# Sums of squares accumulated in PSUM, and a first product twice as wide, in a two-layer diffusion backbone

## The chip, the core and the metric

The kernel runs on one core of one Trainium2 chip. The time is device microseconds of one execution. Five engines work side by side, each through its own queue in order: PE (TensorE, matrix products into PSUM), DVE (VectorE), ACT (ScalarE), POOL (GpSimd), and SP (SyncE, which here issues nearly all DMAs). PEld is the loading of PE's stationary operand.

## The reference

Two layers of a transformer over 512 latent and 256 context tokens of width 1024, all in float32. What matters here is the first thing that layer 0 does:

```python
mod = silu_c @ w_mod[l] + b_mod[l]           # and mod_c for the context stream
sh1, sc1, g1, sh2, sc2, g2 = jnp.split(mod[:, None, :], N_MOD, axis=-1)
h = modulate(rms_norm(x, g_norm_attn[l]), sh1, sc1)
proj = h @ w_in[l]   # query latent 256 | kv latent 128 | rope key 32 | sq 512 | sk 128 | sv 128 | dq 512 | dk 512 | dv 512 | gates 3072
```

`rms_norm` divides every token by the root of the mean of its squares over the 1024 features; the columns of `proj` then feed three attention branches (latent attention, windowed attention, differential attention) and three gates. `dv` are the values of the differential branch.

## The kernel before

The residual is kept transposed: eight feature tiles `x[k]` of 128 features by 768 tokens (latent tokens first, context tokens after them). Products run in float32r: each operand is split into a rounded part and a remainder (`hh`, `hl` for the normed tokens, `wh`, `wl` for weights), and three products are summed in PSUM (hi by hi, hi by lo, lo by hi). A piece of weights comes by DMA into one of two slots `wr` (line 194), ACT rounds it into `wh` (line 197) and POOL subtracts to get `wl` (line 199); both stand in four common slots, or in slots of the phase's own.

The first stage (`first_norm`, `first_products`) goes like this.

1. The eight tiles `x[k]` come by DMA. ACT squares each (lines 322 and 392), DVE adds the squares up in one tile `acc` (line 393).
2. PE sums `acc` over its 128 features (`rows_rsq`, line 402): six products `st`, one per block of 128 tokens, each with a whole 128x128 stationary block of `acc` and two columns to move. A float32 product is two instructions in the trace.
3. DVE takes the inverse root in twelve small steps (lines 443 to 454) and puts it on a diagonal, `dg` (line 405). PE spreads it over all partitions (`nr`, line 339), ACT copies that to `rb` (line 340).
4. Shift and scale of the norm come from `silu(c) @ w_mod`, in four quarters of 2 MB of weights (`mod_first`): 32 small products `pm` per quarter (line 266), a copy `me`, a transpose `pmt` (line 274), two additions on DVE (line 295) and the gains `A` (lines 380, 382).
5. For each feature tile k: `nt` on DVE (line 355), `hh` on ACT (line 357), `hl` on DVE (line 358), then 18 products `pq` (lines 205 to 207) of 128x256: six token tiles by three. They give the query latent, which stays in PSUM over all eight k. The quarter `pm` of the next two feature tiles stands ahead of the even k's products, its transpose `pmt` ahead of the odd k's.

Within this stage PE's instructions stand in the order in which the program writes them (`manual_schedule`); everywhere else a list scheduler orders them by its own estimates.

Then comes the projection phase (`phase1`): the copies of the query latent out of PSUM (line 573); the key and value columns in one chunk of 416 columns (`pb`, lines 481 to 483, weights `wkvs`, 144 products); then chunks of 256 columns, one letter each in the string `mcafldebghijnPk`. A chunk is 144 products, followed by norm and rotation on DVE and stores to DRAM. `f`, `l`, `b` and `h` are short ones (18 products each, latent attention's keys and values), `d` and `j` its queries, `e` and `k` the two halves of the differential values. Two eighths of a further modulation (`mod_units`, products `pm`, weights `wm1` by line 306) follow each letter. Everything after that, from the attention on, is not touched.

Of the kernel before, what the change touches and what calls it, by code (L numbers as in the profile page):

```python
"""Two layers of the hybrid diffusion backbone (MLA + windowed GQA + differential attention).

The residual stream is kept transposed (features on partitions, tokens on the free axis, latent
tokens first, context tokens after them).  Products run in float32r: every float32 operand is split
exactly into a rounded part and a remainder, and the three products that matter at float32
accuracy (hi*hi, lo*hi, hi*lo) are accumulated in PSUM.
"""
# [27 lines left out]
# columns of w_in  # L35
C_QLAT, C_KVLAT, C_KPE, C_SQ, C_SK, C_SV, C_DQ, C_DK, C_DV, C_G = (
    0, 256, 384, 416, 928, 1056, 1184, 1696, 2208, 2720)
# rope order of a head: [first halves of row and column | second halves of row and column]
# [3 lines left out]
# broadcast vectors of a layer  # L42
V_MQ, V_MK, V_SQ, V_SK, V_DQ, V_DK, V_SINK, V_L = 0, 96, 192, 256, 320, 384, 448, 456
NV = 456 + 256
# per-partition vectors of a layer
P_GA, P_GM, P_BM, P_GQ, P_GKV, P_GS = 0, 8, 16, 64, 66, 67
NP_ = 68
# constants
# [30 lines left out]
def _layout(inp):  # L79
    """Host side: permutations and concatenations only."""  # L80
# [6 lines left out]
    # units of four feature blocks: shift and scale of the first norm by pairs of feature tiles, then kinds 2, 4 and 3  # L87
# [49 lines left out]
class Build:  # L137
    def __init__(self, tc, ins, out):
        self.tc = tc
        self.nc = tc.nc  # L140
        self.ins = ins
        self.out = out
        self.n = 0
        self.mq = []
        self.early = False
        self.gains = {}
        self.F1, self.WD, self.WC = 0.3, 1.5, 0.4   # how the gates are spread over the attention
        self.px = 0

# [11 lines left out]
    def R(self, name, dt=F32):  # L161
        """a [128, 768] tile of the phase's pool"""
        return self.ph.tile([128, 768], dt, tag="R", bufs=self.NR, name=self.nm(name))
# [7 lines left out]
    def psx(self, name):  # L171
        """one bank for a dense product, from both tags in turn"""
# [16 lines left out]
    def piece(self, src, n=1024, own=0):  # L189
        """hi, lo of a piece of weights; own: the number of slots it takes of the phase's pool in place of the common  # L190
        ones."""
# [10 lines left out]
    def mm3(self, out, ah, al, bh, bl, start, stop):  # L202
        """out += (ah + al).T @ (bh + bl) but for al.T @ bl."""
# [9 lines left out]
    def dense_steps(self, ps, w, x, c):  # L213
        """ps = sum of w.T @ x[:, c]; w: [(hi, lo)] stationary [128, 128] blocks, x: [(hi, lo)] moving."""
# [8 lines left out]
    def split_sb(self, src, n=768):  # L223
        """hi, lo of an SBUF tile."""
# [7 lines left out]
    def mod_start(self, kinds):  # L232
        """queue up mod = silu(c) @ w_mod + b_mod for the given sixths, features on partitions."""
# [27 lines left out]
    def mod_pe(self, w, ks, ps):  # L261
        """ps[32 g + stream, 128 features] += 2 silu(c) @ w for four feature blocks g; w [128, len(ks), 512]."""
# [7 lines left out]
    def mod_out(self, ps, pt):  # L270
        """[128 features, 4 blocks, 32]: twice the modulation without its bias."""
# [5 lines left out]
    def mod_first(self, q):  # L277
        """shift and scale of the first norm for feature tiles 2q and 2q + 1, in two steps."""
# [18 lines left out]
    def mod_units(self, n):  # L297
        """n pieces of the modulation of kinds 2, 4 and 3 of the first layer."""
# [18 lines left out]
    def first_norm(self, x, h):  # L317
        """the first norm, feature tiles as their modulation arrives, and the query latent of the first layer: PSUM
        tiles [128 tokens, 256]."""
        nc = self.nc  # L320
        acc = self.S("acc0")
        first = nc.scalar.activation(out=acc, in_=x[0], func=AF.Square)
        with self.tc.issue_after(first.ins):
            for k in range(1, KT):
                self.add_square(acc, x[k], k, slice(0, 768), self.P("sq"), nc.vector)
        with self.tc.manual_schedule(engines={mybir.EngineType.PE}):
            return self.first_products(x, h, acc)

    def first_products(self, x, h, acc):
        nc = self.nc  # L330
        g0 = self.mod_first(0)
        next(g0)
        dg = self.rows_rsq(acc, NT, self.kc[:, K_O1024:K_O1024 + 2])
# [7 lines left out]
        w = self.wpieces([self.ins["wb"][0, 0, i] for i in range(2)], 4, 256, 2)  # L341
        out = []
        for _ in range(2):
            t = self.psS("pq")
            out += [t[:, 0:256], t[:, 512:768]]
        out += [self.psd("pq")[:, 0:256] for _ in range(2)]
        for q in range(4):
            nxt = self.mod_first(q + 1) if q < 3 else iter(())
            for k in (2 * q, 2 * q + 1):
                next(nxt, None)  # L350
# [9 lines left out]
                for i in range(NT):  # L360
                    b = slice(i * 128, i * 128 + 128)
                    self.mm3(out[i], h[k][0][:, b], h[k][1][:, b], *w[k], k == 0, k == KT - 1)
        return out

    def norm_gain(self, l, which, s, k=None):
        """128 * g * (1 + scale) per feature (rows_rsq gives 1 / 128); of feature tiles k and k + 1 alone at every even k."""
# [19 lines left out]
    def add_square(self, acc, x, j, c, sq, eng):  # L386
        """acc += x_j ** 2 on columns c; sq: a scratch tile."""
# [7 lines left out]
    def rows_rsq(self, sq, nt, ones, s=None):  # L395
        """sq [128 features, nt * 128 tokens] of squares -> [128, nt * 128]: rsqrt(mean + eps) of the tokens on the
        diagonal of every block, with eps * s ** 2 if the rows are s times too large. ones: column constant 1 / number
        of features."""
        nc = self.nc
        st = self.psm("st")  # L400
        for t in range(nt):
            nc.tensor.matmul(st[:, 2 * t:2 * t + 2], lhsT=sq[:, t * 128:t * 128 + 128], rhs=ones, start=True, stop=True)
# [1127 lines left out]
```

## Time and profile before

| | |
|---|---|
| timed runs | 2545.8, 2549.3, 2554.59 us; median 2549.3 |
| span of the profiled execution | 2547.0 us, 40061 instructions |
| PE, PEld busy | 2432.5 us (96%), 2136.6 us (84%) |
| DVE, ACT, POOL busy | 1537.6 us (60%), 1079.7 us (42%), 915.1 us (36%) |
| PE busy in the first of 40 slices | six tenths; nine tenths or more in nearly all others |
| DMA in the first slice | 280 GB/s, against a mean of 121 GB/s |

The profiled execution's own time beyond its span is not listed; its span is 2.3 us under the median of the timed runs. A busy time of PE is the sum of stretches in which an instruction was under way; since products overlap, how many start in a stretch says more than the busy share. The column PEclk is the granted TensorE clock as a share of 2.4 GHz (0.50 is 1.2 GHz).

### The profile page before, as it was taken

The numbers are of one execution on the slowest core, as the hardware profiler recorded it, in microseconds if no ns is written. First come the engines' busy times: TensorE is split into PE (matmuls) and PEld (weight loads), VectorE is DVE, ScalarE is ACT, GpSimd is POOL, SyncE is SP. The second block draws the span as 40 slices with busy tenths as digits, with TensorE's granted clock in tenths as the row PEclk, the third lists the DMA queues.
The fourth block names the chain that finished last, engine by engine and source line by source line (L and its number), as shares of the span: only waits on it lengthen the run. The fifth ranks groups of instructions, "written<-read, shape, count | busy, mean of one in ns | idle before, by whom it ended". The sixth has DMA issues, their size and how long they took to land. (4 is left out here: it accounts for less than half of the span.)

```text
span 2547.0 us, 40061 instructions
## 1 busy us (share of the span) xinstructions
PE 2432.5 (96%) x15466; PEld 2136.6 (84%) x15466; DVE 1537.6 (60%) x3081; ACT 1079.7 (42%) x2105; POOL 915.1 (36%) x629
## 2 busy tenths in 40 slices
PE   6999999999999998999999989999999999999999
PEld 5989888888888887888888989998878777888888
DVE  6547777878874479872222277777788874621112
ACT  4343566667652233212222244346666632422321
POOL 2434211111115326434333354441222235454543
PEclk9999999999999999999999999999999999999999
DMA  7265322222346225662111122443323344222222
GB/s 280 90 222 203 131 97 84 96 77 94 100 137 226 94 76 171 214 231 75 59 67 66 60 99 86 173 153 95 103 83 118 110 156 155 83 92 99 91 100 83
DMA packets 133182, 307.38 MB, mean 121 GB/s; under 512 B 43264, under 2 KB 49536, under 8 KB 132608
## 3 DMA queue, kind: packets, MB, share of 16 engines
q1 hardware_dynamic: 122624, 281.23, 32.6%
q10 hardware_dynamic: 10368, 23.60, 2.4%
q8 instruction: 122, 2.00, 0.3%
q14 instruction: 68, 0.56, 0.1%
HBM read 252.08 MB, written 52.70 MB: 120 GB/s over the span
## 5 line engine op out<-in xcount | busy, mean ns | idle before, releaser
L199 POOL TENSOR_TENSOR wl<-wr,wh 128x1024 fp32r<-128x1024 f32 (+2 forms) x266 | 652.6, 2457 | 1139.2 <-ACT wh L197 1066.8
L197 ACT ACTIVATE wh<-wr 128x1024 fp32r<-128x1024 f32 (+2 forms) x266 | 279.5, 1052 | 581.2 <-PE mo L219 317.6
L218 PE MATMUL mo<-uh,wh 128*128 128x512 f32 (+1 forms) x832 | 286.4, 344 | 18.6 <-DVE x L1261 13.6
L219 PE MATMUL mi<-hl,wh 128*128 128x512 f32 (+1 forms) x832 | 285.7, 344 | 3.3 <-DVE hl L434 3.3
L220 PE MATMUL mi<-hh,wl 128*128 128x512 f32 (+1 forms) x832 | 285.2, 343 | 0.0
L218 PE MATMUL mi<-hh,wh 128*128 128x512 f32 (+1 forms) x832 | 284.8, 344 | 0.3 <-DVE x L1261 0.3
L219 PE MATMUL mo<-ul,wh 128*128 128x512 f32 (+1 forms) x832 | 283.8, 341 | 0.0
L220 PE MATMUL mo<-uh,wl 128*128 128x512 f32 (+1 forms) x832 | 283.1, 341 | 0.0
L1307 DVE TENSOR_TENSOR ul<-u,uh 128x512 fp32r<-128x512 f32 (+1 forms) x104 | 80.7, 777 | 304.0 <-POOL u L1306 301.7
L1261 DVE SCALAR_TENSOR_TENSOR x<-mo,mod,x 128x512 f32<-128x512 f32 (+1 forms) x208 | 127.9, 625 | 200.6 <-PE mo L220 200.6
L481 PE MATMUL pb<-wh,hh 128*128 128x256 f32 (+1 forms) x832 | 244.2, 294 | 0.0
L482 PE MATMUL pb<-wl,hh 128*128 128x256 f32 (+1 forms) x832 | 243.2, 292 | 0.8 <-POOL wl L199 0.8
L483 PE MATMUL pb<-wh,hl 128*128 128x256 f32 (+1 forms) x832 | 243.3, 293 | 0.0
L218 PE MATMUL g<-hh,wh 128*128 128x512 f32 (+1 forms) x576 | 212.2, 368 | 0.0
L220 PE MATMUL g<-hh,wl 128*128 128x512 f32 (+1 forms) x576 | 211.8, 368 | 0.0
L219 PE MATMUL g<-hl,wh 128*128 128x512 f32 (+1 forms) x576 | 211.5, 367 | 0.0
L868 ACT ACTIVATE pth<-pT 128x512 fp32r<-128x512 f32 (+3 forms) x344 | 154.1, 462 | 101.7 <-PE pT L865 90.4
L218 PEld LDWEIGHTS mo<-uh,wh 128*128 128x128 f32 x832 | 157.3, 189 | 39.1 <-DVE x L1261 14.9
L869 DVE TENSOR_TENSOR ptl<-pT,pth 128x512 fp32r<-128x512 f32 (+3 forms) x344 | 171.9, 516 | 24.8 <-ACT pth L868 22.6
L219 PEld LDWEIGHTS mi<-hl,wh 128*128 128x128 f32 x832 | 157.3, 189 | 23.5 <-DVE hl L434 3.7
L218 PEld LDWEIGHTS mi<-hh,wh 128*128 128x128 f32 x832 | 156.8, 189 | 20.4 <-DVE x L1261 0.5
L220 PEld LDWEIGHTS mi<-hh,wl 128*128 128x128 f32 x832 | 157.3, 189 | 19.8
(243 smaller groups left out, 5932.5 us busy)
## 6 DMA issues: line engine op xcount, KB each, us to landing
wr<-in_wmi SPq DMA_DIRECT2D x64, 512.0 KB, 3.5
wr<-in_wmo SPq DMA_DIRECT2D x64, 512.0 KB, 3.5
wm<-in_wmod SPq DMA_DIRECT2D x56, 512.0 KB, 3.6
wr<-in_wg SPq DMA_DIRECT2D x48, 512.0 KB, 3.6
wr<-in_wb SPq DMA_DIRECT2D x36, 512.0 KB, 4.2
wm<-in_wm SPq DMA_DIRECT2D x28, 512.0 KB, 4.5
wr<-in_wup SPq DMA_DIRECT2D x24, 512.0 KB, 3.5
gd<-gt ACTq DMA_DIRECT2D x24, 384.0 KB, 2.4
```

Source lines behind the costliest of these rows:

```text
L197: nc.scalar.activation(out=hi[:, :n], in_=raw[:, :n], func=AF.Copy)
L199: nc.gpsimd.tensor_tensor(out=lo[:, :n], in0=raw[:, :n], in1=hi[:, :n].bitcast(F32), op=ALU.subtract)
L218: mm(ps, lhsT=wh, rhs=xh[:, c], start=i == 0, stop=False)
L219: mm(ps, lhsT=wh, rhs=xl[:, c], start=False, stop=False)
L220: mm(ps, lhsT=wl, rhs=xh[:, c], start=False, stop=i == n - 1)
L481: mm(ps[:, :n], lhsT=ah[:, cs], rhs=wh, start=k == 0, stop=False)
L482: mm(ps[:, :n], lhsT=ah[:, cs], rhs=wl, start=False, stop=False)
L483: mm(ps[:, :n], lhsT=al[:, cs], rhs=wh, start=False, stop=k == nk - 1)
L868: nc.scalar.activation(out=hv[:, k0:k0 + n, qs], in_=pv, func=AF.Copy)
L869: nc.vector.tensor_tensor(out=lv[:, k0:k0 + n, qs], in0=pv, in1=hv[:, k0:k0 + n, qs].bitcast(F32), op=ALU.subtract)
L1261: self.nc.vector.scalar_tensor_tensor(out=x[j][:, c], in0=ps, scalar=g, in1=x[j][:, c], op0=ALU.mult, op1=ALU.add)
L1307: nc.vector.tensor_tensor(out=b[:, c], in0=u, in1=a[:, c].bitcast(F32), op=ALU.subtract)
```

## The change

The sums of squares no longer meet in an SBUF tile. ACT squares the even feature tiles and DVE the odd ones, and PE sums each square over its features at once, accumulating the eight in the same PSUM tile `st`: 48 products in place of 6. They stand ahead of everything else on PE. The weights of chunk `e` (column chunk 7, half of the differential values) are loaded beside those of the query latent, and the product of the first stage becomes 512 columns wide: per token tile two groups of three 128x256 products, 36 per k in place of 18. The 512 columns are copied out of PSUM to `rq` and `raw`, so chunk `e` of `phase1` has no products left and its stores move to the front of the string. The quarter `pm` of the next feature tiles now stands behind the third token tile of the even k, its transpose behind the sixth.

```diff
 def first_norm(self, x, h):
-    acc = self.S("acc0")
-    first = nc.scalar.activation(out=acc, in_=x[0], func=AF.Square)
-    with self.tc.issue_after(first.ins):
-        for k in range(1, KT):
-            self.add_square(acc, x[k], k, slice(0, 768), self.P("sq"), nc.vector)
     with self.tc.manual_schedule(engines={mybir.EngineType.PE}):
-        return self.first_products(x, h, acc)
+        return self.first_products(x, h)

 def first_products(self, x, h):
+    st = self.psm("st")
+    for k in range(KT):
+        sq = self.P("sq")
+        if k % 2:
+            nc.vector.tensor_tensor(out=sq, in0=x[k], in1=x[k], op=ALU.mult)
+        else:
+            nc.scalar.activation(out=sq, in_=x[k], func=AF.Square)
+        for t in range(NT):
+            nc.tensor.matmul(st[:, 2 * t:2 * t + 2], lhsT=sq[:, t * 128:t * 128 + 128],
+                             rhs=self.kc[:, K_O1024:K_O1024 + 2], start=k == 0 and t == 0, stop=k == KT - 1,
+                             skip_group_check=True)
+    dg = self.diag_rsq(st, NT)
     g0 = self.mod_first(0)
     next(g0)
-    dg = self.rows_rsq(acc, NT, self.kc[:, K_O1024:K_O1024 + 2])
...
-    w = self.wpieces([self.ins["wb"][0, 0, i] for i in range(2)], 4, 256, 2)
+    w, w2 = [], []
+    for i in range(2):
+        w += self.wpieces([self.ins["wb"][0, 0, i]], 4, 256, 2)
+        w2 += self.wpieces([self.ins["wb"][0, 7, i]], 4, 256)
     out = []
     for _ in range(2):
         t = self.psS("pq")
-        out += [t[:, 0:256], t[:, 512:768]]
-    out += [self.psd("pq")[:, 0:256] for _ in range(2)]
+        out += [t[:, 0:512], t[:, 512:1024]]
+    out += [self.psd("pq") for _ in range(2)]
     for q in range(4):
         nxt = self.mod_first(q + 1) if q < 3 else iter(())
         for k in (2 * q, 2 * q + 1):
-            next(nxt, None)
...
             for i in range(NT):
                 b = slice(i * 128, i * 128 + 128)
-                self.mm3(out[i], h[k][0][:, b], h[k][1][:, b], *w[k], k == 0, k == KT - 1)
+                mm, (hh, hl) = nc.tensor.matmul, h[k]
+                for o, (wh, wl) in ((0, w[k]), (256, w2[k])):
+                    p = out[i][:, o:o + 256]
+                    mm(p, lhsT=hh[:, b], rhs=wh, start=k == 0 and not o, stop=False, skip_group_check=True)
+                    mm(p, lhsT=hh[:, b], rhs=wl, start=False, stop=False, skip_group_check=True)
+                    mm(p, lhsT=hl[:, b], rhs=wh, start=False, stop=k == KT - 1, skip_group_check=True)
+                if k % 2 == 0 and i in (2, 5):
+                    next(nxt, None)
...
         if l == 0:
+            self.dv0 = self.Dt("raw")
+            v = self.dv0.rearrange("p (a t d) -> p a t d", a=2, t=6)
             for i in qt:
                 evq(i, pre[i])
+                nc.scalar.activation(out=v[:, :, i, :], in_=pre[i][:, 256:512].rearrange("p (a d) -> p a d", a=2),
+                                     func=AF.Copy)
...
-            raw = chunk256(ci, at)
+            raw = self.dv0 if l == 0 and ci == 7 else chunk256(ci, at)
...
-        for f in ("mcafldebghijnPk", "abcdjehmflgnikP")[l]:
+        for f in ("emcafldbghijnPk", "abcdjehmflgnikP")[l]:
```

PE's queue at the program's start, before: `pm` is the first quarter's modulation, `st` the sums of squares, `nr` the spread inverse root, `pq` the first product.

```order
L266 MATMUL pm_154<-wm_149,sl 32x128 x12
L402 MATMUL st_167<-kc,acc_124 128x2 x6
L266 MATMUL pm_154<-wm_149,sl 32x128 x20
L274 MATMUL pmt_212<-kc,me_213 128x128
L339 MATMUL nr_218<-dg_189,kc 128x512
L339 MATMUL nr_221<-dg_189,kc 128x256
L266 MATMUL pm_242<-wm_240,sl 32x128 x32
L205 MATMUL pq_236<-wh_226,hh_108 128x256
```

The same place now, from the last of the eight squares on; seven rows like the first stand ahead of it.

```order
L335 MATMUL st_126<-kc,sq_183 128x2 x6
L266 MATMUL pm_213<-wm_208,sl 32x128 x32
L274 MATMUL pmt_247<-kc,me_248 128x128
L346 MATMUL nr_253<-dg_206,kc 128x512
L346 MATMUL nr_256<-dg_206,kc 128x256
L374 MATMUL pq_283<-wh_261,hh_108 128x256
L375 MATMUL pq_283<-wl_263,hh_108 128x256
L376 MATMUL pq_283<-wh_261,hl_109 128x256
L374 MATMUL pq_283<-wh_267,hh_108 128x256
L375 MATMUL pq_283<-wl_269,hh_108 128x256
```

The whole first quarter `pm` now stands behind the sums, the second quarter no longer stands between `nr` and `pq`, and the fifth product of the stage already needs the remainder of the second weight piece (`wl_269`).

SP's queue in the projection phase, around the stores of chunk `d` (`qm`), before: `wm` are weights of the further modulation, `wr` weight pieces, `vd` chunk `e`'s stores, `km` the stores of chunk `b`.

```order
L306 DMA wm_2089<-in_wm 128x1024
L742 DMA qm_1879<-rl_1783 128x384
...
L744 DMA qm_1888<-rc_1784 128x192
L306 DMA wm_2100<-in_wm 128x1024
L194 DMA wr_2528<-in_wb 128x1024
L751 DMA vd_2085<-raw_1928 128x768
L751 DMA vd_2087<-raw_1928 128x768
L306 DMA wm_2181<-in_wm 128x1024
```

And now:

```order
L306 DMA wm_2210<-in_wm 128x1024
L194 DMA wr_2783<-in_wuq 128x768
L766 DMA qm_2106<-rl_2010 128x384
...
L768 DMA qm_2115<-rc_2011 128x192
L306 DMA wm_2220<-in_wm 128x1024
L731 DMA km_2195<-ko_2192 128x576
...
L731 DMA km_2208<-ko_2201 128x576
L306 DMA wm_2440<-in_wm 128x1024
```

The stores of `d` and of `b` now stand with one `wm` between them; before, chunk `e`'s stores and several loads stood there too.

## Rows read from the trace of the kernel before

**Rows 1.** Stretches by engine: busy us (instructions under way), PEclk, DMA share, GB/s.

```profile
15.10:22.00 6.90, 6.68 (x76) 5.24 (x76) 2.95 (x13) 0.04 (x1) 0.00 (x0) 1.00 1.06 442
24.00:28.00 4.00, 4.00 (x28) 2.23 (x32) 4.00 (x3) 1.10 (x3) 4.00 (x2) 1.00 1.02 438
30.00:57.00 27.00, 23.51 (x280) 21.74 (x281) 23.82 (x49) 13.55 (x27) 9.17 (x4) 1.00 0.47 183
94.20:98.00 3.80, 0.00 (x0) 0.00 (x0) 3.80 (x12) 0.00 (x0) 0.66 (x1) 0.81 0.42 153
98.00:104.00 6.00, 5.95 (x30) 5.95 (x31) 5.68 (x20) 1.43 (x3) 0.07 (x1) 0.55 0.16 66
```

**Rows 2.** Timeline: start us, us, engine, instructions, idle before and releaser; squares.

```profile
5.94 0.84 ACT L322 ACTIVATE acc<-x 128x768 f32<-128x768 f32 x1 [2.17 <-DMA x<-in_xT]
11.00 3.73 ACT L392 ACTIVATE sq<-x 128x768 f32<-128x768 f32 x4 [0.19 <-DMA x<-in_xT]
9.85 6.27 DVE L393 TENSOR_TENSOR acc<-acc,sq 128x768 f32<-128x768 f32 x6 [1.12 <-ACT sq L392]
```

**Rows 3.** Timeline of PE up to the first product.

```profile
15.16 1.79 PE L266 MATMUL pm<-wm,sl 128*32 128x128 f32 x24 [15.16 <-DVE acc L393]
16.88 2.72 PE L402 MATMUL st<-kc,acc 128*128 128x2 f32 x12
19.53 2.36 PE L266 MATMUL pm<-wm,sl 128*32 128x128 f32 x40
22.29 0.47 PE L274 MATMUL pmt<-kc,me 128*128 128x128 f32 x1 [0.40 <-ACT me L273]
23.98 2.90 PE L339 MATMUL nr<-dg,kc 128*128 128x512 f32 x4 [1.22 <-DVE mod L295]
26.81 2.67 PE L266 MATMUL pm<-wm,sl 128*32 128x128 f32 x64
31.02 0.39 PE L207 MATMUL pq<-wh,hl 128*128 128x256 f32 x1 [0.47 <-DVE hl L358]
```

**Rows 4.** Timeline of PE: the same sums of squares in a later norm.

```profile
652.58 1.40 PE L402 MATMUL st<-kc,sq 128*128 128x2 f32 x12
```

**Rows 5.** Timeline of ACT, POOL and DVE, from the inverse root to the first product.

```profile
22.13 1.99 ACT L197 ACTIVATE wh<-wr 128x1024 fp32r<-128x1024 f32 x2
23.25 5.10 POOL L199 TENSOR_TENSOR wl<-wr,wh 128x1024 fp32r<-128x1024 f32 x2 [22.81 <-ACT wh L197]
26.92 0.38 ACT L340 ACTIVATE rb<-nr 128x256 f32<-128x256 f32 x1 [0.26 <-PE nr L339]
29.27 1.78 ACT L357 ACTIVATE hh<-nt,mod 128x512 fp32r<-128x512 f32 x3 [1.97 <-DVE nt L355]
```

**Rows 6.** Timeline of POOL and DVE at the end of the first stage.

```profile
51.45 4.71 POOL L199 TENSOR_TENSOR wl<-wr,wh 128x832 fp32r<-128x832 f32 x2 [3.03 <-DMA wr<-in_wkvs]
52.02 4.42 DVE L358 SCALAR_TENSOR_TENSOR hl<-nt,mod,hh 128x512 fp32r<-128x512 f32 x2
```

**Rows 7.** Timeline of PE within the first stage: two products of one run, three waits.

```profile
46.50 0.28 PE L205 MATMUL pq<-wh,hh 128*128 128x256 f32 x1
48.10 0.28 PE L207 MATMUL pq<-wh,hl 128*128 128x256 f32 x1
50.24 0.39 PE L205 MATMUL pq<-wh,hh 128*128 128x256 f32 x1 [1.68 <-ACT hh L357]
54.39 0.38 PE L207 MATMUL pq<-wh,hl 128*128 128x256 f32 x1 [0.76 <-DVE hl L358]
56.50 0.39 PE L207 MATMUL pq<-wh,hl 128*128 128x256 f32 x1 [0.47 <-DVE hl L358]
```

**Rows 8.** Timeline of the projection phase: a wait of PE, two stores on SP, an idle DVE.

```profile
156.01 0.64 PE L266 MATMUL pm<-wm,sl 128*32 128x128 f32 x16 [2.45 <-DMA wm<-in_wm]
174.11 0.80 SPq L742 DMA_DIRECT2D qm<-rl  x2
189.73 1.75 DVE L463 TENSOR_REDUCE ss<-sqs 128x24 f32<-128x1536 f32 x1 [13.43 <-ACT sqs L462]
```

More of the change, by code (lines that the diff above doesn't have):

```diff
@@ L317, in first_norm, with first_products @@
     def first_norm(self, x, h):
+        with self.tc.manual_schedule(engines={mybir.EngineType.PE}):
+            return self.first_products(x, h)
+    def first_products(self, x, h):
         nc = self.nc
-        acc = self.S("acc0")
-        first = nc.scalar.activation(out=acc, in_=x[0], func=AF.Square)
-        with self.tc.issue_after(first.ins):
-            for k in range(1, KT):
-                self.add_square(acc, x[k], k, slice(0, 768), self.P("sq"), nc.vector)
-        with self.tc.manual_schedule(engines={mybir.EngineType.PE}):
-            return self.first_products(x, h, acc)
-    def first_products(self, x, h, acc):
-        nc = self.nc
+        st = self.psm("st")
[10 more added lines that the diff above has]
+        dg = self.diag_rsq(st, NT)
         g0 = self.mod_first(0)
         next(g0)
-        dg = self.rows_rsq(acc, NT, self.kc[:, K_O1024:K_O1024 + 2])
         r = self.ph.tile([128, 768], F32, tag="rb", bufs=1, name="rb")
@@ L402, in rows_rsq, with diag_rsq @@
             nc.tensor.matmul(st[:, 2 * t:2 * t + 2], lhsT=sq[:, t * 128:t * 128 + 128], rhs=ones, start=True, stop=True)
+        return self.diag_rsq(st, nt, s)
+    def diag_rsq(self, st, nt, s=None):
+        nc = self.nc
         r = self.rsq_small(st[:, 0:2 * nt].rearrange("p (t o) -> p t o", o=2)[:, :, 0], nt, 1.0, s)
```

## The prediction

> **What bounds the kernel now.** I read the page's busy shares first: PE is the engine that has no room, so only time in which PE stands still, or runs below its rate, can be won. Then the stretches by engine: the only long stretch with PE underused is the start. Until 15 us PE does nothing, and the first product that runs without a break starts at 31.02 us [rows 3]. From 30 to 57 us PE is busy for 23.5 of 27 us [rows 1], and its timeline there shows three waits of 1.68, 0.76 and 0.47 us [rows 7]. So what the change can win is bounded: some of the 31 us ahead of the stage, and 2.9 us inside it. Everything behind the first stage follows from its end.
>
> **Where the start's 31 us go.** ACT squares the first tile from 5.94 to 6.78 us and ends the last square at 14.73; DVE ends the sum at 16.12 [rows 2]. The sums of squares run on PE from 16.88 to 19.60 [rows 3]; call their end S. From S it is 11.4 us to the first unbroken product: the rest of `pm`, the inverse root, `nr`, `rb`, the gains, `nt`, `hh`, `hl`.
>
> **Part 1: 48 sums in place of 6.** A float32 product is two instructions, so before there are 12 and now 96. The 12 take 2.65 us from start to start (16.88 to 19.53), 0.221 us each [rows 3]. In a later norm the same 12 take 1.40 us, 0.117 each [rows 4]: that is the ratio of the two clock levels, 1.2 and 2.4 GHz. So PE ran at 1.2 GHz at 17 us, though the PEclk column says 1.00 there, a figure I take to mean that no change of level had yet been recorded. At 0.221 us the 96 need 21.2 us; the first square is there at 6.8 us, and a square costs 0.84 to 0.93 us on ACT [rows 2] against the 2.65 us of its six sums, so PE is the bound and the squares, half of them on DVE, are hidden. S moves to 6.8 + 21.2 = 28.0 us: **+8.4 us**. Were the clock full throughout, 96 x 0.117 = 11.2 us would do, and the last square (14.7 us) and its 1.4 us would set S = 18.0 at best, -1.6.
>
> Which is it? What the trace shows of the release: from 15.16 to 21.89 PE had `pm`, `st`, `pm` with hardly a gap [rows 1, 3], and `nr` at 23.98 is still slow. It sped up only within the `pm` of 26.81: 28 instructions are under way in 24 to 28 us [rows 1], and its 64 take 2.67 us (0.042 each) where 40 took 2.36 (0.059) [rows 3]. Ahead of that stand 4 us of unbroken `nr` and `pm`. So 6.7 us with the sums in them did not raise the clock, and products of two moving columns are what fills the new start. I take 1.2 GHz throughout. The Trainium skill, TensorE: Matmul & The Clock Gate, Part 1, says that half rate is the default and that sustained matmul activity releases it; read plainly, 21 us of back-to-back products would raise the clock early. By that rule S would be near 20, the first rival below; the row of 15.1 to 22 us speaks against it.
>
> **Part 2: from S to the unbroken product.** The path now is: all 64 `pm` (1.79 + 2.36 = 4.15 us by rows 3), `me` and `pmt` (0.40 + 0.47), `nr` to the second `rb` (23.98 to 27.30, 3.3 us) [rows 3, 5]: S + 8.3. ACT's order then has the rounding of the second weight piece, 1.0 us, and only then the first `hh`, 0.7 us [rows 5]. The remainder of that piece on POOL takes 2.55 us (5.10 for two) from S + 9.4 to S + 11.9, and the fifth product waits for it. DVE's `hl` is needed as well, and it falls into that POOL instruction: two `hl` that started at 52.02 under POOL's `wl` ended only 0.3 us after it, at 56.44 [rows 6]. So unbroken from about S + 12.0, against S + 11.4: **+0.6 us**. Bounds: -1.3 (products start behind `hh`, nothing else in the way) and +2.0 (two more DVE steps blocked for one `wl`).
>
> **Part 3: the clock at the stage's start.** The quarter `pm` that stood between `nr` and `pq` has gone behind the third token tile, so PE rests from S + 7.9 (`nr`'s end) to S + 12, 4 us with two or three products in it. After 3.8 us without work at 94.2 the trace has a mean clock of 0.55 for 6 us, 30 instructions under way [rows 1]: 6 x 0.45 = 2.7 us lost. Before, the stage began at full rate. **+2.0 us**, from 0 to 2.7.
>
> **Part 4: the stage and chunk `e`.** 144 products of 256 columns come in and 144 go out of chunk `e`, at the same pace: 1.60 us for 14 (46.50 to 48.10), 0.114 each [rows 7], 16.4 us on both sides, net 0. What is won are the waits: with 4.1 us of products per k in place of 2.1, DVE (23.8 us busy of 27) [rows 1] is no longer as close behind PE; -2.9. New ones come where a new pair's gains must go through `pmt`, DVE, ACT and DVE within the 4.1 us of the odd k, with four more `wl` on POOL in the way: +1.0 for three turns, up to 2.3 at 0.76 each. **-1.9 us**. The twelve copies out of PSUM on ACT run beside the last k's products.
>
> **Part 5: what is late next.** The second pieces take two of the four common weight slots, so the fourth `wkvs` piece can be rounded only when the stage has ended, and its remainder stands on POOL behind the rope tables. PE has 33 products of 416 columns ahead of it. **+0.5 us**, from 0 to one of POOL's two-piece stretches, 4.7 [rows 6].
>
> **Part 6: chunk `e` as cover.** While `e` ran, DVE finished `d` (stores issued at 174.11) and then sat idle for 13.43 us until `b` reached it [rows 8], so DVE has room. But the `wm` loads stand on SP behind the stores of `d` and `b`, which wait for DVE, and 16.4 us of products that ran meanwhile are gone. One such late `wm` cost 2.45 us at 156 [rows 8]. **+2.0 us**, from 0 to 4.9 (two of them).
>
> **Sum.** 8.4 + 0.6 + 2.0 - 1.9 + 0.5 + 2.0 = +11.6 us. The profiled execution's span is 2547.0, 2.3 us under the median of the timed runs; added to the median 2549.3 the sum gives **2560.9 us**. The ends that belong together: Part 1 at its value with the low ends, 8.4 - 1.3 + 0 - 2.9 = +4.2; with the high ends 8.4 + 2.0 + 2.7 - 0.6 + 4.7 + 4.9 = +22. Since they hardly fall on one side all at once, this case's own range is 2555 to 2568.
>
> **Rival 1: the sums themselves raise the clock.** After about 4 us (as for `nr` and `pm`) 18 instructions are done, the other 78 at 0.117 take 9.1 us: S = 6.8 + 4.0 + 9.1 = 19.9, +0.3. At full clock `pm` and `nr` save half of 4.15 and 2.90 us, so Part 2 is +0.6 - 3.5 = -2.9, and Part 3 is 0. With -1.9, +0.5 and +2.0: -2.0, 2547.3 us. For it: PE is never empty from 6.8 us on. Against it: the 6.7 us above.
>
> **Rival 2: faster.** The full clock is there almost from the first sum, S = 18.0 (-1.6), Part 2 -2.9 - 1.3, Part 4 -2.9, nothing late behind: -8.7, 2540.6 us. It needs the clock within a few sums, which no stretch before 28 us shows; it decides itself at the pace of the first two feature tiles.
>
> **Rival 3: much slower.** All high ends of the forecast, above all two late `wm` loads with the clock falling behind each as it did at 98 us (2.7 us more each): 22.1 + 5.4, about 2577 us. For it: the stores do stand closer; against it: DVE's 13.43 us of room.
>
> **How the numbers follow.** Forecast 0.66, rival 1 0.22, rival 2 0.06, rival 3 0.06. Under about 0.3% (7.6 us) a run of this kernel can't be told from no change: the three runs before spread over 8.8 us. Faster than 2541.7: rival 2 and a little of rival 1, 0.08. Slower than 2556.9: four fifths of the forecast (0.53) and rival 3, 0.59. Between: 0.33. The range reaches over rival 1 to 2545 and up to 2567, leaving out rival 2, rival 3 and the forecast's top.
>
> **What will show it.** In the changed kernel's timeline: eight groups of 12 `st` at 2.65 us apiece, ending near 28 us (near 20: rival 1; near 18: rival 2); the first product that doesn't wait near 40 us, behind a second-piece `wl`; products at a pace of 0.21 us for the first microseconds there; the stage's end near 82 us, with waits of about 1 us in all; a wait at the first product with the fourth `wkvs` remainder; waits for `wm` in the projection phase. The forecast is wrong at its root if the `st` pace is 0.117 us.

## The result, and the profile after

The changed kernel takes 2568.8 us (median of 4 runs, 2564.2 to 2570.8) beside 2549.3 us for the kernel before: ratio 1.0071, 95% interval 1.0052 to 1.0090. Put beside it a second time on another chip (e9 below), it took 2568.7 against 2550.6: 1.0069, 1.0044 to 1.0093. So the change costs about 18 us. The forecast was +11.6; the direction was right, the size too small, and 2568.8 lies above the range.

I read the profile after from the start. PE's timeline, up to the second quarter `pm` (answers [rows 3]; columns as there):

```profile
6.64 20.64 PE L335 MATMUL st<-kc,sq 128*128 128x2 f32 x96 [6.64 <-ACT sq L332]
27.21 3.64 PE L266 MATMUL pm<-wm,sl 128*32 128x128 f32 x64
31.25 0.47 PE L274 MATMUL pmt<-kc,me 128*128 128x128 f32 x1 [0.40 <-ACT me L273]
31.51 2.20 PE L346 MATMUL nr<-dg,kc 128*128 128x512 f32 x4
36.06 0.39 PE L374 MATMUL pq<-wh,hh 128*128 128x256 f32 x1 [2.34 <-ACT hh L366]
39.51 0.58 PE L376 MATMUL pq<-wh,hl 128*128 128x256 f32 x1 [2.94 <-DVE hl L367]
...
43.22 1.96 PE L266 MATMUL pm<-wm,sl 128*32 128x128 f32 x64
```

96 sums in 20.6 us, 0.215 each, without a gap: half pace throughout. They end at 27.2. The products run without a break from 39.5, 12.3 us later. The last row is the second quarter `pm`: it used to run ahead of the products (26.81 in [rows 3]), now it stands among them.

The stretches by engine show what the clock did (busy us and instructions of PE, PEld, DVE, ACT, POOL, then PEclk, DMA share, GB/s; answers [rows 1]):

```profile
6.60:27.20 20.60, 20.56 (x96) 20.56 (x96) 3.83 (x4) 2.53 (x3) 0.00 (x0) 1.00 0.90 359
36.50:43.00 6.50, 3.56 (x17) 3.49 (x16) 4.41 (x6) 2.07 (x3) 3.77 (x2) 0.50 0.76 290
43.50:57.00 13.50, 13.50 (x211) 12.97 (x200) 5.96 (x14) 3.80 (x7) 2.39 (x1) 1.00 0.83 345
```

The 1.00 of the first row can't be a level: the pace there is that of 1.2 GHz. The column knows a clock only from its first change on. From 36.5 to 43 us it is half, and the first 3.7 us of the stage fall into that.

Behind the stage, one wait for the fourth `wkvs` remainder, and then the projection phase. PE's waits there, by what ended them (total us, times, longest us), first of the changed kernel from 126 to 290 us, then of the kernel before from 98 to 291 us (between 290 us and the end of the phase the changed kernel has no further wait over 0.3 us):

```profile
90.05 0.46 PE L502 MATMUL pb<-wl,hh 128*128 128x416 f32 x1 [1.20 <-POOL wl L199]
```

```profile
PE pm L266 <- DMA wm<-in_wm: 5.8, 5, 2.3
PE pt L634 <- DVE rkv L488: 3.9, 1, 3.9
PE tp L804 <- DVE y L474: 3.8, 1, 3.8
```

```profile
PE tp L780 <- DMA ld<-km: 4.0, 1, 4.0
PE pt L610 <- DVE rkv L468: 4.0, 1, 4.0
PE pm L266 <- DMA wm<-in_wm: 2.7, 2, 2.4
```

Two waits are of the same length as before; that for `wm` has doubled. The phase as a whole, of the changed kernel and of the kernel before:

```profile
126.00:308.00 182.00, 171.08 (x1556) 160.32 (x1555) 116.86 (x276) 69.29 (x128) 65.26 (x47) 0.96 0.53 184
```

```profile
98.10:291.00 192.90, 185.39 (x1700) 175.89 (x1701) 119.68 (x279) 74.03 (x136) 69.43 (x49) 0.98 0.52 184
```

PE stands still for 182.0 - 171.1 = 10.9 us in place of 7.5, with 144 products fewer, at a lower mean clock.

One landmark serves for all that follows: `pT`, the first transposition of the attention, where the program is the same again in all kernels. It starts at 290.0 us before and at 307.1 after. What lies behind it takes 2257.0 and 2261.4 us. (The "marker" of three expectations is a DVE instruction 9.5 us behind pT: 299.6 us before, 317.1 in e9, 292.5 in e10, 294.1 in e11.)

### The profile page after: what moved, and what is told of

Read it like the earlier page. It is cut to its first block, busy times and chain, and to the rows that moved or that the text cites. A ratio compares the mean times of both kernels' runs of the same rounds, so it can differ in the third digit from the quotient of the medians.

```text
span 2568.4 us, 40218 instructions
## 1 busy us (share of the span) xinstructions
PE 2457.5 (96%) x15550; PEld 2160.9 (84%) x15550; DVE 1533.1 (60%) x3078; ACT 1076.0 (42%) x2101; POOL 913.1 (36%) x629
## 5 line engine op out<-in xcount | busy, mean ns | idle before, releaser
L1331 DVE TENSOR_TENSOR ul<-u,uh 128x512 fp32r<-128x512 f32 (+1 forms) x104 | 75.3, 726 | 304.0 <-POOL u L1330 297.1
L502 PE MATMUL pb<-wl,hh 128*128 128x256 f32 (+1 forms) x784 | 229.4, 293 | 2.0 <-POOL wl L199 2.0
L501 PE MATMUL pb<-wh,hh 128*128 128x256 f32 (+1 forms) x784 | 230.3, 294 | 0.0
L503 PE MATMUL pb<-wh,hl 128*128 128x256 f32 (+1 forms) x784 | 230.1, 293 | 0.0
L218 PEld LDWEIGHTS mi<-hh,wh 128*128 128x128 f32 x832 | 156.9, 189 | 20.3 <-DVE x L1285 0.5
```

Of the source, the lines that this page charges most:

```text
L218: mm(ps, lhsT=wh, rhs=xh[:, c], start=i == 0, stop=False)
L501: mm(ps[:, :n], lhsT=ah[:, cs], rhs=wh, start=k == 0, stop=False)
L502: mm(ps[:, :n], lhsT=ah[:, cs], rhs=wl, start=False, stop=False)
L503: mm(ps[:, :n], lhsT=al[:, cs], rhs=wh, start=False, stop=k == nk - 1)
L1331: nc.vector.tensor_tensor(out=b[:, c], in0=u, in1=a[:, c].bitcast(F32), op=ALU.subtract)
```

## The experiments

Twelve runs. "pT" and "rest" (the span behind pT) are from each run's profile, "wm" is PE's wait for `wm` in the projection phase, the ratio is to the kernel before on the same chip.

| run | ratio, 95% interval | pT at | rest | wm |
|---|---|---|---|---|
| before | | 290.0 | 2257.0 | 2.7 |
| before again (e3) | 1.0003 (0.9987 to 1.0019) | 285.5 | 2266.7 | 1.9 |
| changed | 1.0071 (1.0052 to 1.0090) | 307.1 | 2261.4 | 5.8 |
| changed again (e9) | 1.0069 (1.0044 to 1.0093) | 307.6 | 2267.4 | 6.8 |
| e1 sums only | 1.0038 (1.0024 to 1.0051) | 299.6 | 2261.1 | 1.2 |
| e2 wide only | 1.0020 (1.0004 to 1.0035) | 296.6 | 2262.2 | 2.0 |
| e4 zeros ahead | 1.0047 (1.0034 to 1.0061) | 302.7 | 2259.0 | 3.6 |
| e5 128-column sums | 1.0018 (1.0003 to 1.0032) | 300.2 | 2261.2 | 6.4 |
| e6 early rounding | 1.0027 (1.0015 to 1.0038) | 296.5 | 2256.3 | 3.1 |
| e7 four wm slots | 1.0017 (1.0005 to 1.0030) | 301.3 | 2260.1 | 0.4 |
| e12 quarter back | 1.0038 (1.0023 to 1.0054) | 297.6 | 2257.3 | 3.7 |
| e8 before, two fixes | 0.9994 (0.9981 to 1.0006) | 289.3 | 2257.7 | 0.8 |
| e10 before, all fixes | 0.9982 (0.9967 to 0.9997) | 282.7 | 2259.9 | 0.0 |
| e11 changed, all fixes | 0.9977 (0.9964 to 0.9990) | 284.6 | 2257.0 | 0.4 |

The kernel before alone spread over 2543 to 2560 us in 23 runs, so ratios hold to two or three tenths of a per cent; single terms are read from the traces.

**The two halves of the change (e1, e2).** e1 is the kernel before with the diff's loop of `st` sums. e2 is the changed kernel with the old `acc` and six sums; its edit, against the changed kernel:

```diff
...
-            for t in range(NT):
-                nc.tensor.matmul(st[:, 2 * t:2 * t + 2], lhsT=sq[...], ..., start=k == 0 and t == 0, stop=k == KT - 1)
...
+        dg = self.rows_rsq(acc, NT, self.kc[:, K_O1024:K_O1024 + 2])
```

> The kernel before with the 48 accumulated sums in place of SBUF sum and 6 sums; the first product and chunk e as before. Theory A (the sums cost PE time at 1.2 GHz and nothing else): groups of 12 st at about 2.6 us, S near 27.3 us, everything behind later by the same 7.7 us: 2557 us (2554 to 2560), and waits for wm in the projection phase as before (2.7 us). Theory B (a later start costs again behind it, because the later stages come to their gaps with another clock): 2562 us or more. Theory C (the wide product alone made the loss): under 2552 us.

> The changed kernel with the SBUF sum and 6 sums restored; wide product and chunk e at the front stay. Theory A, summing what the changed kernel's trace shows: S back at 19.6, path to the unbroken product +1.2, half clock in the first 3 us of the stage +1.7, waits of the stage -2.6, fourth wkvs piece +1.2, later wm loads and lost cover in the projection phase +4.5: +6, that is 2555 us (2552 to 2559). Rival (the wide product by itself pays, the loss is all the sums'): 2547 to 2549 us. Both edits together gave 2568.8; if they add up, e1 and e2 minus twice the kernel before come near +13 to +19.

Over the mean of before's two profiles (pT at 287.8), e1 is later by 11.8 us and e2 by 8.8; both together (the changed kernel and its repeat, mean 307.3) by 19.6. The totals add up. The single times say the same with wide margins: +0.38% and +0.20% against +0.7%. But they don't add up term by term, so the agreement is in part luck.

e1's 2561.5 lies 1.5 us above theory A's range and just under B's figure, and neither theory has it all. Its sums end at 27.55 us, 8.4 later than before (A said 7.7); but not everything behind follows by the same amount. The way to the unbroken product is 0.8 us longer, and the stage itself 2.4, with the clock at half for its first 5.8 us: a price behind the sums, as in B, though it lies in the first stage and not in the later ones. Its projection phase is no longer than before.

e2's 2558.5 is inside its range, at the upper end, but with other terms than those of its expectation. The projection phase, priced at +4.5, is only 1.6 us longer than before less chunk `e`. The fourth `wkvs` piece, priced at +1.2, makes PE wait for 3.2 us, with 3.4 us at half clock around it, and between the end of the stage and the first `pt` 6.7 us are lost in all:

```profile
83.51 0.71 PE L496 MATMUL pb<-wl,hh 128*128 128x416 f32 x1 [3.22 <-POOL wl L199]
```

**Is there a price behind pT? (e3, e9)** Both kernels once more, unchanged.

> The kernel before, unchanged: a second profile of the same program. Theory A (where the clock falls at a gap behind the first phase differs from one execution to the next): its stretches at half clock, 12 in the first profile with a mean clock of 0.988, differ in number or place, single runs have mean clocks from 0.985 to 0.989, and their spans follow the clock by about 2.5 us per 0.001. Theory B (the gaps of this program always lose the clock in the same places, the changed kernel's in others): the same stretches again, 0.988 in all runs.

> The changed kernel once more, beside the kernel before on this chip, since its first comparison rested on 4 runs and the other kernels ran on other chips. Theory A (the loss lies ahead of 300 us, in the terms that the single edits showed): ratio 1.005 to 1.007, the marker of the attention's first products near 315 us as in the first profile, the rest 2244 to 2254. Rival (the first comparison was high by chance): ratio 1.003 or less.

Against before's first profile the changed kernel's rest was 4.4 us longer, which would have been a quarter of the loss. The second profile of before has a rest longer by 9.7 us than its first. The clock falls or doesn't fall at the same gaps; here is one, in the changed kernel, and the same piece of the program in the kernel before:

```profile
670.00:690.00 20.00, 18.00 (x108) 15.29 (x107) 15.15 (x32) 9.77 (x21) 2.37 (x1) 0.91 0.29 106
```

```profile
655.00:675.00 20.00, 17.97 (x118) 15.19 (x117) 16.45 (x35) 11.65 (x26) 2.37 (x1) 1.00 0.30 106
```

PE is busy for 18.0 us in both, at 0.91 in one and 1.00 in the other. Theory A of e3 holds, and no price behind pT is shown: over two profiles of each kernel the rest differs by 2.5 us, and two profiles of one kernel by 9.7. The 19.6 us up to pT make up the whole measured loss. e9's ratio is within its theory A; its marker came 2 us later than said, and what lies behind that took 2257.9 us, above the 2244 to 2254 given. The side guess of e3, that spans follow the clock at 2.5 us per 0.001, holds only roughly (2542 us at 0.988 and 2557 at 0.987).

**Why the sums stay at half pace (e4, e5).** e4 puts 14 products of 512 zeros ahead of the changed kernel's sums; e5 has no zeros and lets each of the sums move 128 columns.

```diff
+        for i in range(14):
+            nc.tensor.matmul(zp, lhsT=z[:, 0:128], rhs=z, start=True, stop=True)   # e4
...
-                nc.tensor.matmul(st[:, 2 * t:2 * t + 2], ..., rhs=self.kc[:, K_O1024:K_O1024 + 2], ...)
+                nc.tensor.matmul(st[:, 128 * t:128 * t + 128], ..., rhs=self.kc[:, K_O128:K_O128 + 128], ...)   # e5
```

> The changed kernel with 14 products of 512 zero columns on PE ahead of the first sum, from about 1 to 7 us; their result is not used. Theory A (products of two moving columns neither raise nor hold the clock): it is up to 2.4 GHz when the sums begin, the first one or two groups of 12 take near 1.4 us, then 2.65 us again; S at 23 to 27 us, total 2562 to 2568. Rival (once up, the clock stays as long as PE has instructions): all groups near 1.4 us or at the pace of the squares, S near 18 to 19, pm and nr at full rate too, total 2555 to 2559.

> The changed kernel, each of its 48 sums with 128 moving columns of a constant in place of 2 (same number of instructions and weight loads, same result). Theory A (moving columns are what raises the clock; two-column sums kept it at 1.2 GHz, as the warm run showed): the pace goes from 0.22 to about 0.12 us within the first few groups of 12, S near 18 (16 at best: last square 14.7 + 1.4), total 8 to 12 us under the changed kernel: 2557 to 2561. Rival (the weight load sets the pace whatever the clock, or 128 columns cost more than the clock gives back): pace 0.2 us or more, S 27 or later, 2567 to 2572.

Three stretches of e4:

```profile
7.50:10.80 3.30, 3.30 (x32) 3.30 (x31) 1.69 (x2) 1.00 (x2) 0.00 (x0) 1.00 0.99 371
11.00:27.90 16.90, 16.90 (x125) 16.60 (x129) 4.59 (x15) 1.33 (x2) 0.00 (x0) 0.50 0.84 348
28.00:34.70 6.70, 2.35 (x15) 1.04 (x7) 5.04 (x9) 3.76 (x6) 5.10 (x2) 1.00 0.20 66
```

The clock was up by 7.5 us, behind 6 us of zeros, and the first 32 sums ran at 0.1 us each. Then it fell to half, though PE was busy for every one of the 16.9 us; it came back at 27.9, when `pm` with its 128 columns had run since 24.7. So a full queue on PE did not hold the clock here. The Trainium skill, TensorE: Matmul & The Clock Gate, Part 1, says that sustained matmul activity releases the clock. This trace does not agree for sums of two columns: 64 instructions of them ran at half rate from 10.9 to 24.7 us without a gap. The total fell as theory A said, to 2563.4.

And two stretches of e5:

```profile
6.60:12.40 5.80, 5.78 (x27) 5.78 (x28) 1.92 (x2) 1.10 (x2) 0.00 (x0) 1.00 0.99 366
12.50:20.30 7.80, 7.80 (x72) 7.68 (x70) 1.92 (x2) 1.33 (x2) 0.00 (x0) 1.00 1.06 433
```

27 instructions in 5.8 us (0.21 each), then about 70 in 7.8 (0.11): the same 96 instructions with sixty-four times the columns, and the clock came. The sums end at 20.3 in place of 27.2 (I had said near 18), about 1 us behind the SBUF sum's 18.8 and 19.5; the total, 2557.7, is within theory A's range. (e5 to e8 ran on a chip where the kernel before took 2554.4 us, 3 to 5 more than on the others; their ratios are the better measure.)

**From the sums to the products (e6, e12).** e6 rounds the first two weight pieces while the sums run; e12 puts the second quarter `pm` back between `nr` and the products.

```diff
+        w = self.wpieces([self.ins["wb"][0, 0, 0]], 4, 256, 2)        # e6, ahead of me
+        w2 = self.wpieces([self.ins["wb"][0, 7, 0]], 4, 256)
+        with self.tc.issue_after(self.last_wh):
+            next(g0, None)
...
+            if q == 0:                                                # e12, ahead of k = 0
+                next(nxt)
```

> The changed kernel with ACT's rounding of the first two weight pieces ahead of me (while the sums run) and so POOL's remainders ahead of the norm's end. Theory A (from S to the unbroken product the way was 12.4 us because rounding stood ahead of hh, and DVE's gains and hl fell into POOL's wl): S as before, 27.2; A on DVE 0.2 us in place of 2.4, unbroken product at S + 9 to S + 10, total 2564 to 2566. Rival (pm, me, pmt, nr, rb set the way): S + 12 again, 2568.

> The changed kernel with the second quarter pm (64 instructions) back between nr and the first products, where PE otherwise rests; nothing else. Theory A (the forecast left out that this quarter's products, hidden before, now stand in the stage, 2.0 us by its row): first transposition of the attention (pT) 2 us earlier than in the changed kernel's two profiles (307.1, 307.6), near 305; the clock still falls, since PE's wait of 2.9 us for hl stays. Theory B (it also keeps the clock up): 1.9 us more, near 303. Rival (in the stage the quarter stood in DVE's waits and cost nothing): 307, with 2 us more of waits between the first and the last pq. Total by A 2566, by B 2564; the traces decide.

In the changed kernel DVE and POOL between `dg` and the first products stand like this:

```profile
32.15 2.44 DVE L398 TENSOR_SCALAR A<-A 128x2 f32<-128x2 f32 x2
34.51 4.29 DVE L364 SCALAR_TENSOR_TENSOR nt<-x,A,rb 128x512 f32<-128x512 f32 x4
...
32.22 2.35 POOL L199 TENSOR_TENSOR wl<-wr,wh 128x1024 fp32r<-128x1024 f32 x1 [31.77 <-ACT wh L197]
35.21 2.64 POOL L199 TENSOR_TENSOR wl<-wr,wh 128x1024 fp32r<-128x1024 f32 x1 [0.64 <-ACT wh L197]
```

The two gains of two columns took 2.44 us, as long as POOL's `wl` beside them; four `nt` took 4.29 with the second `wl` beside them, and `hl` comes behind those. The same with early rounding (e6), PE above, DVE below:

```profile
34.81 0.38 PE L375 MATMUL pq<-wh,hh 128*128 128x256 f32 x1 [1.80 <-ACT hh L367]
35.77 0.38 PE L377 MATMUL pq<-wh,hl 128*128 128x256 f32 x1 [0.47 <-DVE hl L368]
...
32.14 0.24 DVE L399 TENSOR_SCALAR A<-A 128x2 f32<-128x2 f32 x2
```

And its stretch behind the first products (columns as above):

```profile
35.80:42.30 6.50, 6.50 (x101) 6.17 (x102) 1.88 (x5) 2.69 (x5) 3.56 (x2) 1.00 0.86 340
```

The gains take 0.24 us, the products run unbroken from 35.8 (S + 8.4, a little under theory A's S + 9), and at full clock: PE waits 0.47 us for `hl` in place of 2.94. pT comes 10.8 us earlier: 3.7 at the start, 1.9 that the clock had cost, and the rest in the projection phase, where `wm` waits fell by 3 us and the time at half clock by 6.5. The total, 2561.1, is 3 us under theory A's range.

e12's quarter runs in PE's rest, and the wait for `hl` stays, as theory A said:

```profile
32.61 1.96 PE L266 MATMUL pm<-wm,sl 128*32 128x128 f32 x64 [0.26 <-ACT rb L347]
38.89 0.38 PE L378 MATMUL pq<-wh,hl 128*128 128x256 f32 x1 [2.96 <-DVE hl L369]
```

The clock still falls as well, for 3.4 us of the stage; e1, which has this quarter in the rest too, lost it for 5.8 us with a wait of 2.95. So it was the wait for `hl`, not the missing quarter, that had to go (e6). From the unbroken product to the last `pq` it takes 39.9 us, 42.6 in the changed kernel: the quarter's 2.0 and 0.7 more. But pT comes 9.7 us earlier, not 2 to 4: five of them in the projection phase again. So A's term is shown, its total (2566, measured 2561.7) was wrong.

**Why wm loads are late (e7).**

```diff
-                with self.phase("p1", ND=5, NPB=3, NM=2):
+                with self.phase("p1", ND=5, NPB=3, NM=2 if l else 4):
```

> The changed kernel with four slots for the wm loads of the projection phase in place of two. Theory A (wm loads are late because each waits for a slot behind the stores on SP): PE's waits for wm in the phase fall from 5.8 us to under 1.5, total near 2564. Rival (they are late because the stores ahead of them on SP wait for DVE, slots don't matter): waits of 4 to 6 us again, 2568.

PE's waits in the projection phase of e7:

```profile
PE pt L634 <- DVE rkv L488: 4.0, 1, 4.0
PE tp L804 <- DMA ld<-km: 3.6, 1, 3.6
PE pm L274 <- ACT me L273: 2.2, 1, 2.2
...
PE pm L266 <- DMA wm<-in_wm: 0.4, 1, 0.4
```

`wm` waits are gone, so theory A holds for what those loads waited for: a slot. 2.2 us came back as a wait for a copy on ACT. The total, 2560.8, is 3 us under theory A's figure. That two slots are always too few without the cover of `e` is not shown, as the phase from the first `pt` to pT shows in all these kernels (us; PE's time without work, time at half clock and `wm` waits within it; the kernel before without chunk `e`'s 16.4 us):

| | phase | PE still | half clock | `wm` |
|---|---|---|---|---|
| before, twice | 175.6, 173.5 | 7.5, 6.5 | 8.8, 6.5 | 2.7, 1.9 |
| changed, twice, and e5 | 181.4, 182.1, 182.1 | 10.9, 11.8, 11.7 | 13.2, 13.5, 13.7 | 5.8, 6.8, 6.4 |
| e4 | 179.6 | 9.7 | 13.7 | 3.6 |
| e2, e6, e12 | 176.1, 176.5, 176.7 | 8.4, 8.4, 8.6 | 6.8, 6.8, 6.8 | 2.0, 3.1, 3.7 |
| e7 | 175.7 | 6.8 | 12.9 | 0.4 |

e2, e6 and e12 have two slots and no cover, and their phase is within 1 us of e7's. Against the changed kernel e7 won PE's standing still and kept the half clock; these three won most of the half clock and part of the standing still. The same in stretches, e7 and then e12:

```profile
125.60:301.30 175.70, 168.95 (x1548) 159.77 (x1548) 121.80 (x279) 69.06 (x127) 67.38 (x47) 0.96 0.51 183
```

```profile
120.90:297.50 176.60, 168.04 (x1547) 157.00 (x1548) 117.89 (x279) 69.02 (x127) 65.58 (x47) 0.98 0.55 188
```

**Versions that put it together (e8, e10, e11).** e8 is the kernel before with 128-column accumulated sums and early rounding of both its pieces. e10 adds the zeros ahead, four slots, and takes the remainder of the first pieces from POOL to DVE:

```diff
-        nc.gpsimd.tensor_tensor(out=lo[:, :n], in0=raw[:, :n], in1=hi[:, :n].bitcast(F32), op=ALU.subtract)
+        eng = nc.vector if self.dve_lo else nc.gpsimd
+        eng.tensor_tensor(out=lo[:, :n], in0=raw[:, :n], in1=hi[:, :n].bitcast(F32), op=ALU.subtract)
```

e11 is the changed kernel with the same and with e12's quarter.

> The kernel before (256 columns wide, chunk e in its place) with the 128-column accumulated sums and the early rounding of its two weight pieces. If both theories A above hold: S at 17 to 18 in place of 19.5, unbroken product at about 26.5 in place of 31, first stage at full clock, total 4 to 5 us under the kernel before: 2546 to 2547. Rival (what the start wins is given back in the stage, where DVE is the bound): 2550 to 2552.

> The kernel before (256 columns, chunk e in its place) with all that the runs showed to help: 14 products of zeros ahead, 128-column accumulated sums, first weight piece rounded early with its remainder on DVE instead of POOL (e8 lost 5 us to POOL's remainders ahead of DVE's gains), four wm slots. Theory: full clock from 7.5 us on, S near 17, unbroken product at 25 to 27 (31 before), wm waits under 1: marker near 290 us (295 to 300 before), total 5 to 8 us under the kernel before, ratio 0.997 to 0.998. Rival (the stage, DVE-bound, returns it): unbroken product early, marker 295 or later, ratio 0.9995 or more.

> The changed kernel with the same: zeros ahead, 128-column sums, two pieces rounded early with remainders on DVE, a quarter pm back between nr and pq, four wm slots. Theory (the wide product by itself wins its 2.6 us of stage waits and loses as much behind): marker within 3 us of e10, ratio 0.997 to 0.999. Rival 1 (the wide product has a price left, lost cover): marker 5 us or more behind e10, ratio 1.000 or more. Rival 2 (it pays once its side costs are gone): marker 3 us or more ahead of e10.

e8 failed in its own way: 2551.1 is within its rival's range, but not for the rival's reason, since the loss lies ahead of the stage. Its sums end at 20.0 (17 to 18 expected), its products start at 33.3 (26.5 expected). At 20.0 the inverse root begins, and within a microsecond POOL starts its two remainders. DVE's inverse root, POOL, and PE's `nr`:

```profile
20.75 0.17 DVE L464 TENSOR_TENSOR a<-y 128x6 f32<-128x6 f32 x1
20.95 2.22 DVE L465 SCALAR_TENSOR_TENSOR a<-a,v 128x6 f32<-128x6 f32 x1
23.20 2.26 DVE L466 SCALAR_TENSOR_TENSOR y<-a,y 128x6 f32<-128x6 f32 x1
...
20.75 4.69 POOL L199 TENSOR_TENSOR wl<-wr,wh 128x1024 fp32r<-128x1024 f32 x2 [20.31 <-ACT wh L197]
...
27.80 2.90 PE L348 MATMUL nr<-dg,kc 128*128 128x512 f32 x4 [5.10 <-DVE mod L295]
```

Two instructions on six columns, 0.17 us each elsewhere, took 2.2 us each, one per remainder: 4.1 us lost, in the inverse root (e10's expectation says 5 us and puts them at the gains). The Trainium skill, SBUF — State Buffer, Who interferes with whom, says that a DVE instruction with two inputs in SBUF contends with a GpSimd one that reads SBUF, and that the ports they share are an exclusive lock. The rows agree: each of the two DVE instructions lasts about as long as one remainder (4.69 us for two). So early rounding helps when the sums are slow (e6: POOL done at 25.5, before S) and hurts when they are fast (e8).

e10 and e11 mend that. e10's start:

```profile
6.88 10.98 PE L342 MATMUL st<-kc,sq 128*128 128x128 f32 x96 [0.90 <-ACT sq L339]
17.80 2.12 PE L268 MATMUL pm<-wm,sl 128*32 128x128 f32 x64
...
27.37 0.39 PE L207 MATMUL pq<-wh,hh 128*128 128x256 f32 x1
```

Sums at 0.114 us from the start, S at 17.8 (17 expected), products at 27.4 (25 to 27), the marker at 292.5 (290). Times 2545.6 and 2545.5 beside 2550.6: both faster than the kernel before, by 0.2% with intervals that just keep clear of 1. Their pT lie 1.9 us apart: with its side costs gone, the wide product wins nothing and costs nothing that these runs can tell, which was e11's theory. In the traces e11's stage is 4.4 us shorter than e10's with chunk `e`'s 16.4 added; 2.6 us of that go ahead of the stage, 1.9 between it and the first `pt`, and 1.8 in the projection phase.

## Why the forecast was right and wrong, step by step

Each term, from the means of two profiles of each kernel (the first one and its repeat):

| step | forecast | measured | from |
|---|---|---|---|
| Part 1, 96 sums | +8.4 | +8.0 | end of `st` 27.2; before 19.5 and 18.8 |
| Part 2, S to products | +0.6 | +0.8 | 12.3 against 11.5 |
| Part 3, half clock | +2.0 | +1.9 | 3.7 and 4.0 us of the stage at half |
| (second quarter `pm` in the stage) | 0 | +2.0 | 1.96 at 43.22; e12 |
| Part 4, waits of the stage | -1.9 | -2.6 | idle 0.3 and 0.5 against 3.0 and 3.0 |
| Part 5, fourth `wkvs` piece | +0.5 | +1.0 | 1.2 and 0.9 |
| Part 6, projection phase | +2.0 | +7.2 | `pt` to pT 181.4 and 182.1; before, less 16.4, 175.6 and 173.5 |
| behind pT | 0 | +2.5 | two profiles of before differ by 9.7 |
| sum up to pT | +11.6 | +18.3 | pT itself: +19.6; time: about +18 |

The rows don't make up all of pT's 19.6. Some 0.8 of the missing 1.3 us is the wait before the first `pt`, 2.3 us in before's second profile and 3.9 to 4.0 in the other three; the rest is not placed.

Parts 1 and 2 were right, and for the reasons given: the sums at 1.2 GHz throughout (0.215 us each, against rival 1; e4 and e5 show what it hangs on), and products near 40 us, behind DVE work that lay under a second-piece remainder. The stage's end, forecast near 82, came at 82.2. Part 3 had the right size and only half the reason: the clock fell, but in e12, with the quarter back in the rest, and in e1, where it never left the rest, it fell as well. The wait of 2.9 us for `hl` is enough for it, and without that wait (e6) the clock stayed up.

The step that failed is Part 6: "+2.0 us, from 0 to 4.9 (two of them)". It measured +7.2. Two things were wrong in it. I took the one late `wm` of before as the measure and allowed for two; there were five and seven, 5.8 and 6.8 us in all. And I priced them as waits only. PE stood still 4.3 us more than before (10.9 and 11.8 against 7.5 and 6.5), and the time at half clock grew from 8.8 and 6.5 us to 13.2 and 13.5, another 2.9 us. About half of that stands behind a late load: after

```profile
185.10 0.65 PE L266 MATMUL pm<-wm,sl 128*32 128x128 f32 x16 [2.29 <-DMA wm<-in_wm]
```

the clock was at half from 186.6 to 190.0 us. The other half stands around the last long wait of the phase, ahead of `tp`, which is 4 us in both kernels: 6.8 us at half in place of 3.4. A late load does not always cost the clock: behind before's wait of 2.45 us at 156 [rows 8] it stayed up,

```profile
155.00:165.00 10.00, 8.99 (x79) 8.40 (x80) 4.87 (x17) 5.78 (x12) 1.44 (x2) 1.00 0.81 287
```

and e7 has 12.9 us at half with hardly a late load. The clock behind a late load stood only in rival 3, at 0.06. The argument against, DVE's 13.43 us of room [rows 8], missed the point: the late loads waited for slots, as e7 shows.

A smaller miss sits in Part 3 too. I saw that the second quarter `pm` had left PE's rest and priced the rest by its clock, but not the quarter itself: 64 instructions that had been hidden now run among the products, 2.0 us.

What stays open is why the projection phase varies as it does. With two slots and no cover, `wm` waits were 5.8, 6.8 and 6.4 us in three profiles (changed twice, e5) and 2.0 to 3.7 in four (e2, e4, e6, e12), though the program of that phase is the same and only its start moves. e6 and e12 gained five microseconds there that neither of their edits touches, and in e2, e6 and e12 the phase cost 1.6 to 2.2 us, what Part 6 said. So slots explain what the late loads waited for, and not why there were more of them in the changed kernel than in these three.

## What to carry to other kernels

Read the pace of the first products and not only PE's busy share: here 96 instructions of two columns kept PE busy for 20.6 us at the pace of 1.2 GHz, while the same 96 with 128 columns took 13.75 (e5), and 10.98 behind throwaway products (e10). When a change takes away work that stood in front of a stream of loads, count the slots of that stream, and allow for a fall of the clock behind a late load. When instructions are moved out of a rest, price them twice: the rest that they leave, and the place where they now stand. And when two halves of a change add up in total, check that they do so term by term.

## What the runs showed of the hardware

- TensorE's clock fell from 2.4 to 1.2 GHz under back-to-back float32 products of two columns: full from 7.5 to 10.9 us, half from 10.9 on, through the end of the sums at 24.7 to 27.9, PE never idle (e4). With 128 columns the same 96 instructions raised it by 12.4 us (e5).
- The column of the granted clock reads 1.00 ahead of its first change, whatever the clock is: 0.21 us per instruction there, 0.11 behind it (e5).
- A DVE instruction of 0.17 us lasted 2.2 us when it met POOL's float32 subtraction, and the next one, of 2.26 us, met the next subtraction (e8).
- The clock fell behind waits of PE for a load of 2.29 us (changed kernel), 2.22 (e5) and 1.80 (e4), and not behind one of 2.45 us (before, at 156).
- One program's executions differ in where the clock falls: two profiles of the kernel before have 61 and 75 us at half clock in all, and 23 runs of it on one chip spread over 16 us.
